# A two-layer decoder trunk on one NeuronCore: the fourth token sum of each FFN issued piece by piece in the first chain of the seven-product stage, one down-projection slot moved from the third chain to the end

## The chip, the cores and the metric

The kernel runs on one core of one Trainium2 chip. The metric is device time in microseconds (us), the median over several runs. Engines are named as in the profile: PE (TensorE matmul), PEld (its weight loads), DVE (VectorE), ACT (ScalarE), POOL (GpSimd), SP (SyncE, which here only issues transfers). Each engine takes its own instructions in the order in which they were issued.

## The reference

Two layers over 512 tokens of width 1024, in float32. Layer 0 mixes tokens by dilated attention, layer 1 by a gated linear recurrence; behind each mixer comes a gated convolutional FFN, and RMS norms stand around every part. The change touches the FFN only:

```python
def conv_ffn(x, w_up, conv_w, conv_b, w_down):
    u = causal_dwconv(x @ w_up, conv_w, conv_b)      # width 2 * 3072, a convolution of 3 tokens
    g, v = u[..., :D_FF], u[..., D_FF:]
    return (jax.nn.gelu(g, approximate=True) * v) @ w_down

def reference(x, ...):
    for layer in range(2):
        ...
        h = rms_norm(x, norm_ffn_pre[layer])
        h = conv_ffn(h, ffn_w_up[layer], ffn_conv_w[layer], ffn_conv_b[layer], ffn_w_down[layer])
        x = x + rms_norm(h, norm_ffn_post[layer])
    return x
```

## The kernel before

**Split products.** Every float32 operand is split into a high part (a copy by ACT, L149) and a low part (raw minus high, by DVE, L150). A product is then three matmuls: high by high, high by low, low by high.

**Two stages of the up-projection.** The 12 column blocks of the up-projection have two halves of 256 columns each, the gate half and the value half. Blocks 0 and 1 are done plainly (`feat_tiles`, `tiles`, matmuls of L412). Blocks 2 to 11 are done in `seven` as 20 *chains*, one for each half block. A chain multiplies a 2 by 2 arrangement of weight blocks and token blocks with seven products instead of eight; that needs sums of weight blocks and sums of token blocks. The four token sums are made once in each FFN by `token_sums`, a generator that is advanced by one step at each tick: `whole` adds high and low part again (tiles `B`, L938), differences follow (L944, L956, L963), and `parted` splits the result into the tiles `T` (ACT L149, DVE L150). The fourth sum, `T[3]`, is read by one product only, number 4.

**Slots.** The order of work in `seven` is written out by hand. A chain has ten places, `CYCLE = 10`, and the next chain starts ten places later; `AT = {1: 0, 5: 1, 2: 2, 6: 4, 3: 5, 7: 8, 4: 13}` gives the place of each product, so product 4 of a chain falls between two products of the next one. A place with something in it is a slot, called by its number m: m = 0 is product 1 of the first chain, m = 4 its product 6, m = 5 its product 3, m = 8 its product 7, m = 13 its product 4. A product is 12 matmuls with 256 columns (L1022). The places 6 and 7 of each chain (for the first two chains place 7 alone), and two places behind the last chain, hold `rows`: a part of the down-projection, 6 matmuls with 512 columns (L412, tiles `acc`). `free_slots` lists these 40 places, and the 40 parts are laid on them in order.

**What a slot issues.** `slot` issues the slot's matmuls, then what earlier slots left to be done `later`, then a `tick`. A tick first advances the generators on the side (`token_sums` here) and then, unless `state["hold"]` is set, calls `pump`, which splits the next weight piece (ACT L149, tiles `whi`; DVE L150, tiles `wlo`). In this stage a tick pumps one piece. `state["live"]` counts the piece buffers in use, of 16. The list of pieces has also the DVE additions that form the weight sums, `across` (L210) and `lower` (L214), and the transfers by POOL that add to a weight block (L186).

**What the seven products leave.** The products 1, 6, 7 and 4 of a chain add up in one half of a PSUM bank, 5, 3 and 2 in another bank. Behind the products 1, 6 and 5 ACT copies the running sum out into a tile `part` (L1031) before the next product is added onto it: so product 6 waits for the copy behind product 1, product 7 for the copy behind product 6, and product 3 for the copy behind product 5. DVE adds `part` to the finished bank (L1035 for the upper half of the result, L1040 for a part of the lower one; product 4 waits for L1040), and then come the bias (ACT L773), two taps of the convolution (DVE L777), and the gelu (ACT L795) or the gate (DVE L799).

**Ticks of the token sums.** Twelve ticks pass in blocks 0 and 1; the slots of `seven` go on counting. In the kernel before, the twelfth tick issues `whole` and both differences of the fourth sum (L938 twice, L944 twice), and the tick of slot m = 0 issues its two splits.

Of the kernel before, what the change touches and what calls it, by code (L numbers as in the profile page):

```python
# [32 lines left out]
HALVES = 16  # L33
# [8 lines left out]
CYCLE = 10  # L42
# [41 lines left out]
def kernel(  # L84
# [63 lines left out]
    def split(hi, lo, raw):  # L148
        nc.scalar.activation(hi, raw, AF.Copy)  # L149
        nc.vector.tensor_tensor(lo, raw, hi.bitcast(F32), op=ALU.subtract)  # L150
# [41 lines left out]
    def free_slots(n):  # L192

        end = CYCLE * n
        free = [CYCLE * c + r for c in range(n) for r in ((6, 7) if c > 1 else (7,))] + [end, end + 1]
        assert not {CYCLE * c + a for c in range(n) for a in AT.values()} & set(free)
        return free

# [104 lines left out]
    def pump(limit=2):  # L303

        for _ in range(limit):
            if not pieces:
                refill()
            while pieces and pieces[0][0] is None:
                pieces.pop(0)[1]()
            if not pieces or pieces[0][0][0] >= state["dma"]:  # L310
                continue
            if state["live"] + 2 - single(pieces[0][0][1]) <= HALVES:
                key, cuts, last = pieces.pop(0)
                cuts = cuts()
                his, los = [], []
                for n, raw in enumerate(cuts):
                    hi, lo = (
                        wp.tile([P] + list(raw.shape[1:]), F32R, tag=t, name=nm("w" + t)) for t in ("hi", "lo")
                    )
                    split(hi, lo, raw)  # L320
                    his.append(hi)
                    los.append(lo)
                units[key] = (his, los)
                state["live"] += len(cuts)
                state["used"] += last
                while pieces and pieces[0][0] is None:
                    pieces.pop(0)[1]()
            while not state["quiet"] and state["dma"] < len(plan) and state["dma"] - state["used"] < RAW_BUFS:
                load()
# [35 lines left out]
    def slot(emit, length=1):  # L365
        emit()
        for d in list(due):
            d[0] -= 1
            if d[0] < 0:
                due.remove(d)  # L370
                d[1]()
        tick(length)
# [544 lines left out]
    def token_sums(hT, T, first=False):  # L917

        if not first:
            assert len(sides) == 1, len(sides)  # L920
            d = dp.tile([P, 4, D], F32, name=nm("x_kept"))
            nc.gpsimd.dma_start(d, X[0])
            kept.append(d)
        homes = cp.tile([P, 4, D], F32R, tag="x_sb", name=nm("T"))
        homes = [homes[:, n] for n in range(4)]
        homes += [cp.tile([P, D], F32R, tag="gain", name=nm("T"), bufs=2) for _ in range(1 if first else 2)]
        homes = [[h[:, 0:512], h[:, 512:1024]] for h in homes]
        if first:
            homes += [[gen(F32R, "T") for _ in range(2)]]
        homes += [[wp.tile([P, 512], F32R, tag=t, name=nm("T")) for _ in range(2)] for t in ("hi", "lo")]  # L930
        state["live"] += 2
        homes = [[h.rearrange("p (k t) -> p k t", k=2) for h in hs] for hs in homes]
        yield 1 + first

        def both(k0, n):
            o = gen(s="B").rearrange("p (k t) -> p k t", k=2)
            hi, lo = (h[:, k0 : k0 + 2, n * 256 : n * 256 + 256] for h in hT)
            tt(o, hi.bitcast(F32), lo.bitcast(F32), op=ALU.add)  # L938
            return o

        tt = nc.vector.tensor_tensor

        def negative(o, a, b):
            nc.vector.scalar_tensor_tensor(o, a, -1.0, b, op0=ALU.mult, op1=ALU.subtract)  # L944

        def whole(k0, n):
            return [both(k0 + 2 * k, n) for k in range(2)]

        def parted(n, b):
            for k in range(2):  # L950
                split(homes[2 * n][k], homes[2 * n + 1][k], b[k])

        b11, b12 = whole(0, 0), whole(0, 1)
        yield 1 + first
        for k in range(2):
            tt(b11[k], b11[k], b12[k], op=ALU.subtract)  # L956
        parted(0, b11)
        yield 1 + first
        b22 = whole(4, 1)
        if not first:  # L960
            yield 1
        for k in range(2):
            tt(b12[k], b22[k], b12[k], op=ALU.subtract)  # L963
            negative(b22[k], b11[k], b22[k])
        yield 1 + first
        parted(1, b22)
        T.extend([homes[2 * n], homes[2 * n + 1]] for n in range(4))
        yield 1 + first
        parted(2, b12)
        yield 1 + first  # L970
        b21 = whole(4, 0)
        if first:
            yield 2
        for k in range(2):
            negative(b21[k], b22[k], b21[k])
        yield 1 + first
        parted(3, b21)

    LEFT = {5: ("s1", 1), 1: ("w11", 0), 3: ("s4", 1), 2: ("w12", 0), 6: ("s2", 1), 7: ("s3", 1), 4: ("a22", 1)}

# [65 lines left out]
    def seven(hT, T, begin, prep):  # L1046

        right = rights(hT, T)
        i0, acc, ends_at = state["next"], {}, CYCLE * 2 * len(SEVEN)

        def finish(b, ps, j, minus=False):
            later(2, begin(b, ps, j, minus, True))

        def ends(j, half):
            return (
                lambda ps: later(0, lambda: finish(2 * half, ps, j)),
                lambda ps: finish(2 * half + 1, ps, j, True),
            )

        def rows(k, pair):  # L1060
            W, A = take(i0, ("rows", k)), take(i0, ("act", k))
            for t in pair:
                if t not in acc:
                    acc[t] = psum("acc")
                mm3(acc[t], [a[0][:, t * P : (t + 1) * P] for a in A], [w[0] for w in W], not k, False)
            if pair[-1] == 3:
                done(2)

        fill = [lambda k=k, p=p: rows(k, p) for k in range(REST[0]) for p in ((0, 1), (2, 3))]
        steps = {}  # L1070
        n = 0
        for j in SEVEN:
            for half in range(2):
                f = chain(right, *ends(j, half))
                steps.update((CYCLE * n + AT[p], f(p)) for p in AT)
                n += 1
        free = free_slots(n)
        assert len(free) == len(fill)
        steps.update(zip(free, fill))
        state["even"] = True  # L1080
        for m in range(max(steps) + 1):
            if m == ends_at - 2:
                prep()
            if m in steps:
                slot(steps[m])
        while due:
            slot(lambda: None)
        done(2)
        state["even"] = False
        return acc  # L1090
# [626 lines left out]
```

## Time and profile before

| | |
|---|---|
| median of 3 runs | 1430.27 us (1430.02 to 1430.35) |
| the profiled execution: its own time | 1431.97 us |
| its span | 1430.1 us |
| mean granted PE clock | 0.994 |
| PE busy | 1405.7 us (98% of the span) |
| DVE busy | 1140.5 us (80%) |
| ACT busy | 800.2 us (56%) |
| POOL busy | 235.4 us (16%) |
| `seven` of layer 0, first product to the end of the last | 535.85 to 800.58 us |
| `seven` of layer 1, the same | 1081.68 to 1346.56 us |

Rows of the timeline read: start, length, engine, line, operation, output<-input, count, and in brackets how long the engine sat idle before it and for what. Rows of the chain of waits read: start, length, what. Rows of the windows give for each stretch its length, then for PE, PEld, DVE, ACT and POOL the busy time and (in brackets) the number of instructions, then the granted PE clock (1.00 is full), the share of the DMA engines and GB/s.

### The profile page before, as it was taken

The page shows a single profiled execution, that of the slowest core. Times are in us where ns is not written, and L with a number is a line of the kernel's source. Part 1 is how long each engine was busy: PE and PEld are TensorE (multiplying, and loading weights), DVE is VectorE, ACT ScalarE, POOL GpSimd, SP SyncE. Part 2 cuts the span into 40 slices and gives each one's busy share as a digit, 9 for nine tenths or more (in the row PEclk, how much of TensorE's full clock was granted, in tenths as well). Part 3 has the DMA queues.
Part 4 walks back from the last instruction along what each step waited for, and adds up shares of the span by engine and source line. Part 5 has one row for each costly group of instructions (what it writes and reads, how often), then busy time and mean ns, then how long its engine had stood idle before and what let it go on. Part 6 is the DMA issues. An engine that isn't in the chain of part 4 may idle for free.

```text
span 1430.1 us, 23824 instructions
## 1 busy us (share of the span) xinstructions
PE 1405.7 (98%) x8885; PEld 1275.0 (89%) x8885; DVE 1140.5 (80%) x2229; ACT 800.2 (56%) x1670; POOL 235.4 (16%) x352
## 2 busy tenths in 40 slices
PE   9999999999999998999999999999998999999997
PEld 7888999999998888999999889888897999999886
DVE  6676898787855988988888758779789898888843
ACT  7343555363636555666666555588455656666641
POOL 0341333130400211222110001000101112211000
PEclk9999999999999999999999999999999999999999
DMA  7553455664756545666664632432354666665511
GB/s 225 180 146 105 131 166 151 171 178 144 190 171 218 167 116 108 153 155 148 148 125 119 221 118 89 134 117 89 119 155 93 137 147 155 147 151 119 183 57 59
DMA packets 176108, 204.03 MB, mean 143 GB/s; under 512 B 10688, under 2 KB 145304, under 8 KB 175736
## 3 DMA queue, kind: packets, MB, share of 16 engines
q1 hardware_dynamic: 123064, 153.34, 33.5%
q0 software_dynamic: 52080, 48.11, 18.7%
q8 instruction: 70, 1.15, 0.3%
q10 hardware_dynamic: 848, 1.05, 0.2%
q14 instruction: 46, 0.38, 0.1%
HBM read 183.51 MB, written 18.96 MB: 142 GB/s over the span
## 4 chain that ended last, share of the span: by engine, by line
PE 84%; DVE 9%; ACT 5%; issue 1%; DMA 1%; POOL 0%; DVEq 0%; SPq 0%; ACTq 0%
PE ps L1022 38%; PE acc L412 24%; PE ps L412 9%; PE v L1215 7%; DVE wlo L150 2%; DVE u L777 2%; PE v L1153 1%; DVE xb L1520 1%; ACT whi L149 1%; PE O L1427 1%; PE S L1361 1%; PE S L1309 1%; DVE B L938 1%; ACT sig L1541 1%; PE tr L502 1%
## 5 line engine op out<-in xcount | busy, mean ns | idle before, releaser
L150 DVE TENSOR_TENSOR wlo<-raw,whi 128x512 fp32r<-128x512 f32 x632 | 417.5, 686 | 111.8 <-ACT whi L149 109.0
L149 ACT ACTIVATE whi<-raw 128x512 fp32r<-128x512 f32 x632 | 371.3, 625 | 141.9 <-PE ps L1022 45.9
L1022 PE MATMUL ps<-T,whi 128*128 128x256 f32 x1792 | 329.6, 284 | 14.8 <-ACT part L1031 11.0
L1022 PEld LDWEIGHTS ps<-T,whi 128*128 128x128 f32 x1792 | 280.6, 191 | 20.6 <-ACT part L1031 11.4
L1022 PE MATMUL ps<-T,wlo 128*128 128x256 f32 x896 | 252.0, 281 | 0.0
L1022 PE MATMUL ps<-hT,whi 128*128 128x256 f32 x1344 | 250.1, 284 | 0.0
L412 PE MATMUL ps<-hT,whi 128*128 128x512 f32 (+1 forms) x960 | 248.3, 348 | 0.0
L1022 PEld LDWEIGHTS ps<-hT,whi 128*128 128x128 f32 x1344 | 210.7, 192 | 0.8
L1022 PE MATMUL ps<-hT,wlo 128*128 128x256 f32 x672 | 190.9, 284 | 0.0
L412 PEld LDWEIGHTS ps<-hT,whi 128*128 128x128 f32 x960 | 167.6, 189 | 22.2
L186 POOL DMA_DIRECT2D raw<-in_ffn_w_up_dram x80 | 102.9, 1312 | 455.5 <-DVE wlo L150 337.2
L1022 PEld LDWEIGHTS ps<-T,wlo 128*128 128x128 f32 x896 | 171.5, 191 | 0.0
L412 PE MATMUL ps<-hT,wlo 128*128 128x512 f32 (+1 forms) x480 | 166.4, 347 | 0.0
L412 PE MATMUL acc<-whi,ahi 128*128 128x512 f32 x352 | 137.4, 390 | 0.0
L412 PE MATMUL acc<-whi,alo 128*128 128x512 f32 x352 | 137.2, 390 | 0.2
L412 PE MATMUL acc<-wlo,ahi 128*128 128x512 f32 x352 | 137.0, 389 | 0.0
L1022 PEld LDWEIGHTS ps<-hT,wlo 128*128 128x128 f32 x672 | 129.5, 193 | 0.0
L1031 ACT ACTIVATE part<-ps 128x256 f32<-128x256 f32 x168 | 63.8, 380 | 96.1 <-PE ps L1022 91.1
L1215 PE MATMUL v<-whi,hT 128*128 128x512 f32 x320 | 106.5, 396 | 0.0
L412 PEld LDWEIGHTS ps<-hT,wlo 128*128 128x128 f32 x480 | 90.8, 189 | 11.4
L777 DVE SCALAR_TENSOR_TENSOR u<-ps,cols,u 128x511 f32<-128x511 f32 x112 | 83.6, 746 | 4.9 <-ACT u L773 2.9
L773 ACT ACTIVATE u<-ps,cols 128x512 f32<-128x512 f32 x56 | 43.5, 776 | 70.8 <-DVE ps L1035 64.5
(206 smaller groups left out, 2165.3 us busy)
## 6 DMA issues: line engine op xcount, KB each, us to landing
raw<-in_ffn_w_up_dram SPq DMA_DIRECT2D x48, 1024.0 KB
raw<-in_attn_w_qkv_dram SPq DMA_DIRECT2D x67, 512.0 KB
raw<-in_ffn_w_up_dram POOLq DMA_DIRECT2D x80, 256.0 KB, 4.8
raw<-in_ffn_w_down_dram SPq DMA_DIRECT2D x14, 1024.0 KB
dw<-in_ffn_w_down_dram SPq DMA_DIRECT2D x40, 256.0 KB
raw<-in_lru_w_in_dram SPq DMA_DIRECT2D x8, 1024.0 KB
turned<-T POOLq DMA_DIRECT2D x26, 256.0 KB, 2.6
ft<-turned POOLq DMA_DIRECT2D x104, 64.0 KB, 4.4
```

Of the source, the lines that this page charges most:

```text
L149: nc.scalar.activation(hi, raw, AF.Copy)
L150: nc.vector.tensor_tensor(lo, raw, hi.bitcast(F32), op=ALU.subtract)
L186: nc.gpsimd.dma_start(to, src, accum_op=ALU.add)
L412: mm(dst, l[a], r[b], start=start and n == 0, stop=stop and n == 2)
L502: nc.tensor.transpose(ps[:, k * P : (k + 1) * P], xs[i][:, k * P : (k + 1) * P], ident)
L773: nc.scalar.activation(u, ps, AF.Identity, scale=own[:, j : j + 1], bias=cc[:, 48 + j : 49 + j])
L777: nc.vector.scalar_tensor_tensor(u[:, d:], ps[:, : S - d], wc, u[:, d:], op0=ALU.mult, op1=ALU.add)
L938: tt(o, hi.bitcast(F32), lo.bitcast(F32), op=ALU.add)
L1022: mm(dst, W[wa][0][:, k, :], right[n](ha, k), start=n in (1, 5) and k == q == 0, stop=k == 3 and q == 2, skip_group_check=True,)
L1031: later(1, lambda: nc.scalar.activation(to, dst, AF.Copy))
L1153: mm(banks[t], hT[a][:, k, t * P : (t + 1) * P], W[b][k % 2][:, 0, :], start=u == n == 0, stop=u == 3 and n == 5,)
L1215: mm(bank, hT[a][:, k, t * P : (t + 1) * P], W[b][k % 2][:, 0, :], start=(k, a, b) == (0, 0, 0), stop=(k, a, b) == (KD - 1, 1, 0),)
```

## The change

Three things, in both FFN layers:

1. In `token_sums` (for the FFN only; the attention's call, `first=True`, issues what it did) the two differences and the two splits of the fourth sum are no longer issued two at a time at the twelfth tick and the tick of m = 0. They go out one by one: the differences at m = 2 and m = 5, the splits at m = 8 and m = 11. In each of these four ticks `hold` is set, so no weight piece is split there.
2. `free_slots` gives the third chain one place for `rows` instead of two (place 26 goes), and there is a third place behind the last chain. All later parts of `rows` stand one place further on, their pieces and loads with them.
3. From m = 25 on, a slot whose number divides by five pumps one piece more, as long as fewer than 14 piece buffers are in use.

```diff
@@ free_slots @@
-        free = [CYCLE * c + r for c in range(n) for r in ((6, 7) if c > 1 else (7,))] + [end, end + 1]
+        free = [CYCLE * c + r for c in range(n) for r in ((6, 7) if c > 2 else (7,))] + [end, end + 1, end + 2]
@@ token_sums @@
         b21 = whole(4, 0)
+        yield 2 if first else 3
+        for k in range(2):
+            if not first:
+                state["hold"] = True
+            negative(b21[k], b22[k], b21[k])
+            if not first:
+                yield 1
+                state["hold"] = False
+                yield 1
         if first:
             yield 2
+            parted(3, b21)
+            return
         for k in range(2):
-            negative(b21[k], b22[k], b21[k])
-        yield 1 + first
-        parted(3, b21)
+            state["hold"] = True
+            split(homes[6][k], homes[7][k], b21[k])
+            yield 1
+            state["hold"] = False
+            yield 1
@@ seven @@
             if m in steps:
                 slot(steps[m])
+                if m > 2 * CYCLE and m % 5 == 0 and state["live"] < HALVES - 2:
+                    pump(1)
```

ACT at the start of `seven` in layer 0, from the first product on (`T1199` and `T1200` are the high parts of `T[3]`, `part1252` and `part1253` before, `part1251` and `part1252` now, are the copies behind the first chain's products 1 and 5, the second row of the first of them the one behind product 6; `u` is a convolution result). Before:

```order
L149 ACTIVATE whi1246_6296<-raw1189_5928 128x512
L149 ACTIVATE whi1249_6302<-raw1189_5928 128x512
L149 ACTIVATE T1199_5997<-B1244_6290 128x512
L149 ACTIVATE T1200_5998<-B1245_6292 128x512
L149 ACTIVATE whi1254_6326<-raw1133_5649 128x512
L1031 ACTIVATE part1252_6320<-ps1251_6307 128x256
L149 ACTIVATE whi1258_6348<-raw1207_6009 128x512
L1031 ACTIVATE part1253_6321<-ps1257_6334 128x256
L149 ACTIVATE whi1260_6366<-raw1189_5928 128x512
L149 ACTIVATE whi1262_6383<-raw1189_5928 128x512
L1031 ACTIVATE part1252_6320<-ps1251_6307 128x256
```

Now (the lines stand 13 further down, L1031 is L1044):

```order
L149 ACTIVATE whi1246_6294<-raw1189_5928 128x512
L149 ACTIVATE whi1248_6298<-raw1189_5928 128x512
L149 ACTIVATE whi1253_6318<-raw1133_5649 128x512
L1044 ACTIVATE part1251_6316<-ps1250_6303 128x256
L149 ACTIVATE whi1258_6342<-raw1207_6009 128x512
L1044 ACTIVATE part1252_6317<-ps1257_6328 128x256
L149 ACTIVATE whi1260_6373<-raw1189_5928 128x512
L1044 ACTIVATE part1251_6316<-ps1250_6303 128x256
L149 ACTIVATE whi1264_6401<-raw1189_5928 128x512
L773 ACTIVATE u1266_6417<-ps1257_6328,cols251_1206 128x512
L149 ACTIVATE T1199_5997<-B1244_6290 128x512
L149 ACTIVATE whi1270_6439<-raw1189_5928 128x512
```

The two splits into `T` stood ahead of the first copy `part`, and now stand behind the third one; `T1200` follows two rows below the last one shown, behind one more copy `part`. `whi1260`, which reads the result of the DVE addition L210, still stands ahead of the copy behind product 6.

DVE at the same place, from the fourth sum's `whole` on (`B1244` and `B1245`; `T1201` and `T1202` are the low parts of `T[3]`). Before:

```order
L938 TENSOR_TENSOR B1244_6290<-hT01043_5292,hT11044_5293 128x512
L938 TENSOR_TENSOR B1245_6292<-hT01043_5292,hT11044_5293 128x512
L944 SCALAR_TENSOR_TENSOR B1244_6290<-B1220_6123,B1244_6290 128x512
L944 SCALAR_TENSOR_TENSOR B1245_6292<-B1221_6125,B1245_6292 128x512
L150 TENSOR_TENSOR wlo1247_6297<-raw1189_5928,whi1246_6296 128x512
L150 TENSOR_TENSOR wlo1250_6303<-raw1189_5928,whi1249_6302 128x512
L799 TENSOR_TENSOR u1231_6202<-u1231_6202,u1243_6286 128x512
L150 TENSOR_TENSOR T1201_5999<-B1244_6290,T1199_5997 128x512
L150 TENSOR_TENSOR T1202_6000<-B1245_6292,T1200_5998 128x512
L150 TENSOR_TENSOR wlo1255_6327<-raw1133_5649,whi1254_6326 128x512
L210 TENSOR_TENSOR raw1189_5928<-raw1189_5928 128x4x128
```

Now, from behind `whole` (L1035 is L1048, L1040 is L1053):

```order
L150 TENSOR_TENSOR wlo1254_6319<-raw1133_5649,whi1253_6318 128x512
L210 TENSOR_TENSOR raw1189_5928<-raw1189_5928 128x4x128
L150 TENSOR_TENSOR wlo1259_6343<-raw1207_6009,whi1258_6342 128x512
L944 SCALAR_TENSOR_TENSOR B1244_6290<-B1220_6123,B1244_6290 128x512
L150 TENSOR_TENSOR wlo1261_6374<-raw1189_5928,whi1260_6373 128x512
L214 TENSOR_TENSOR raw1189_5928<-raw1189_5928 128x4x128
L944 SCALAR_TENSOR_TENSOR B1245_6292<-B1221_6125,B1245_6292 128x512
L1048 TENSOR_TENSOR ps1257_6328<-ps1257_6328,part1251_6316 128x512
L150 TENSOR_TENSOR wlo1265_6402<-raw1189_5928,whi1264_6401 128x512
L150 TENSOR_TENSOR T1201_5999<-B1244_6290,T1199_5997 128x512
L1053 TENSOR_TENSOR ps1250_6303<-ps1250_6303,part1252_6317 128x256
```

Between `whole` and `L210` eight instructions stood and now four (two `wlo`, L799 and `wlo1254`); behind the last row shown follow the two L777 of `u1266`, `wlo1271` and only then `T1202`.

PE at the end of `seven` in layer 0. Before, the last rows ahead of the last chain's product 4 (`T_5997` and `T_5999` are parts of `T[3]`):

```order
L412 MATMUL acc_6554<-whi_9267,whi_9285 128x512
L412 MATMUL acc_6554<-wlo_9268,whi_9285 128x512
L412 MATMUL acc_6554<-whi_9267,wlo_9286 128x512
L412 MATMUL acc_6558<-whi_9267,whi_9285 128x512
L412 MATMUL acc_6558<-wlo_9268,whi_9285 128x512
L412 MATMUL acc_6558<-whi_9267,wlo_9286 128x512
L1022 MATMUL ps_9289<-T_5997,whi_9305 128x256
L1022 MATMUL ps_9289<-T_5999,whi_9305 128x256
```

Ahead of these eight rows stand six more of L412 and then, before, the last chain's product 7. Now there are 18 rows of L412 between the products 7 and 4 instead of 12; the first of them are:

```order
L412 MATMUL acc_6537<-whi_9214,whi_9233 128x512
L412 MATMUL acc_6537<-wlo_9215,whi_9233 128x512
L412 MATMUL acc_6537<-whi_9214,wlo_9234 128x512
L412 MATMUL acc_6541<-whi_9214,whi_9233 128x512
L412 MATMUL acc_6541<-wlo_9215,whi_9233 128x512
L412 MATMUL acc_6541<-whi_9214,wlo_9234 128x512
L412 MATMUL acc_6392<-whi_9275,whi_9295 128x512
```

No instruction is added or removed on any engine, and the order on POOL and SP stays as it was.

## The prediction

> **What bounds the kernel now.** I read the page's busy shares and chain of waits first, then PE's waits, then the timeline where they lie.
>
> ```profile
> PE 1405.7 (98%) x8885; PEld 1275.0 (89%) x8885; DVE 1140.5 (80%) x2229; ACT 800.2 (56%) x1670; POOL 235.4 (16%) x352
> ...
> PE 84%; DVE 9%; ACT 5%; issue 1%; DMA 1%; POOL 0%; DVEq 0%; SPq 0%; ACTq 0%
> ```
>
> PE is busy for 98% of the span. The change neither adds nor removes matmuls, so it can win only PE's idle time (24 us) and stretches at a low clock. PE's waits, summed over the kernel (total, times, longest):
>
> ```profile
> PE ps L1022 <- ACT part L1031: 11.0, 2, 5.5
> PE ps L1022 <- DVE ps L1040: 3.8, 3, 1.3
> ```
>
> The wait of 5.5 us comes once in each FFN, at the start of `seven`, and one of 1.3 us once in each FFN at its end (the third is in the attention). The start in layer 0, from the timeline of PE, DVE and ACT:
>
> ```profile
> 537.61 1.14 ACT L149 ACTIVATE whi<-raw 128x512 fp32r<-128x512 f32 x2
> ...
> 540.01 0.28 PE L1022 MATMUL ps<-hT,wlo 128*128 128x256 f32 x1
> 540.34 1.53 DVE L777 SCALAR_TENSOR_TENSOR u<-ps,cols,u 128x511 f32<-128x511 f32 x2
> 541.78 1.28 DVE L938 TENSOR_TENSOR B<-hT,hT 128x512 f32<-128x512 f32 x2
> 542.99 1.29 DVE L944 SCALAR_TENSOR_TENSOR B<-B,B 128x512 f32<-128x512 f32 x2
> 543.70 1.23 ACT L149 ACTIVATE T<-B 128x512 fp32r<-128x512 f32 x2 [4.95 <-DVE B L944]
> 544.19 1.29 DVE L150 TENSOR_TENSOR wlo<-raw,whi 128x512 fp32r<-128x512 f32 x2
> 544.84 0.61 ACT L149 ACTIVATE whi<-raw 128x512 fp32r<-128x512 f32 x1
> 545.36 0.36 ACT L1031 ACTIVATE part<-ps 128x256 f32<-128x256 f32 x1
> ...
> 545.78 0.80 PE L1022 MATMUL ps<-T,whi 128*128 128x256 f32 x2 [5.49 <-ACT part L1031]
> ...
> 547.80 0.69 DVE L210 TENSOR_TENSOR raw<-raw 128x512 f32<-128x512 f32 x1
> ...
> 548.52 1.15 ACT L149 ACTIVATE whi<-raw 128x512 fp32r<-128x512 f32 x2 [2.00 <-DVE raw L210]
> ...
> 551.07 0.63 PE L412 MATMUL acc<-whi,whi 128*128 128x512 f32 x1
> ...
> 552.74 0.40 PE L1022 MATMUL ps<-T,whi 128*128 128x256 f32 x2
> ...
> 558.44 0.40 PE L1022 MATMUL ps<-T,whi 128*128 128x256 f32 x2
> ...
> 559.88 0.40 PE L1022 MATMUL ps<-T,whi 128*128 128x256 f32 x2
> ```
>
> ACT had nothing to do from 538.75 on but stood 4.95 us before the split of the fourth token sum, because DVE was late with its differences. The copy `part` behind product 1, which PE needs for product 6, stood behind that split. So a sum that is read only at m = 13 (558.44) held up product 6 at m = 4. Layer 1 shows the same:
>
> ```profile
> 1091.61 0.80 PE L1022 MATMUL ps<-T,whi 128*128 128x256 f32 x2 [5.49 <-ACT part L1031]
> ```
>
> The wait costs more than its length. Windows (PE busy, PEld, DVE, ACT, POOL, then the granted clock), and two rows of the chain of waits for a chain at full clock:
>
> ```profile
> 540.30:545.80 5.50, 0.02 (x1) 0.03 (x1) 5.46 (x10) 2.10 (x5) 0.00 (x0) 0.92 0.00 0
> 545.80:551.10 5.30, 5.30 (x25) 5.30 (x26) 5.18 (x9) 2.72 (x7) 1.28 (x1) 0.50 0.36 111
> ...
> 576.70:589.50 12.80, 12.80 (x98) 12.31 (x97) 11.47 (x20) 8.54 (x16) 2.77 (x3) 1.00 0.68 148
> ```
>
> ```profile
> 577.02 9.99 PE ps L1022 x84
> 587.01 2.75 PE acc L412 x12
> ```
>
> A product slot lasts 9.99/7 = 1.43 us at full clock, a slot of `rows` 2.75/2 = 1.38. From 545.78 to 552.74 lie two products and one `rows`: 6.96 us instead of 4.24, so 2.7 us went to half clock. The wait costs 5.49 + 2.7 = 8.2 us in each layer.
>
> **The change, part by part.** First the start. Nothing ahead of DVE's L938 at 541.78 changes. DVE moves on by 0.60 us for each 512-wide instruction (541.78 to 542.99 for two), by 0.72 for each L777 (540.34 to 541.78 for two).
>
> *Product 6* needs the copy behind product 1. On ACT only one `whi` now stands ahead of it after 538.75, so it is done by 538.75 + 0.6 + 0.4 = 539.8, ahead of PE's 540.29 (540.01 + 0.28). The old wait is gone, and with it the low clock.
>
> *Product 7* needs the copy behind product 6, which stands on ACT behind `whi1260`, which waits for DVE's L210. Ahead of L210 are now `whole` and four instructions instead of eight: L210 at 541.78 + 6 x 0.60 = 545.4, against 547.80. From L210 to `whi` it was 0.72 us (547.80 to 548.52), from a `whi` to the copy behind it 0.52 (544.84 to 545.36), from copy to PE 0.42 (545.36 to 545.78): product 7 can start at 547.05. PE would be there at 540.29 + 2 x 1.43 + 1.38 = 544.5. **A new wait of 2.5 us**, with ACT idle in it. Late behind it on ACT are the next piece and `u` of L773; PE's next user of those is the second chain, which is pushed back by the same 2.5 us.
>
> One more row is needed for the next step, `u` by its group (busy, mean ns of one):
>
> ```profile
> L773 ACT ACTIVATE u<-ps,cols 128x512 f32<-128x512 f32 x19 | 14.8, 780 | 32.2 <-DVE ps L1035 32.2
> ```
>
> *Product 4* of the first chain needs `T[3]`. On DVE stand behind L210, at 0.60 each: `wlo1259` 546.0, L944, `wlo1261`, L214, L944, L1048 at 549.0, `wlo1265`. ACT's `u` (L773) follows L1048 at 549.7 and takes 0.78 (780 ns), then `T1199` to 551.1; DVE then does `T1201` (551.15), L1053 (551.75, 0.33 to the next, as in the row at 798.58 below), two L777 to 553.55, `wlo1271`, and `T1202` from 554.15 to 554.85. PE reaches product 4 at 547.05 + 4 x 1.43 = 552.8; seven of its matmuls (0.12 each) run before the first that reads `T1202`, so it stands from 553.6 to 554.9: **1.3 us more**. It ends at 554.9 + 0.6 = 555.5. Before, the slot behind it began at 559.88.
>
> So each start wins 559.88 - 555.5 = **4.4 us** (8.2 less 2.5 and 1.3). I followed the pieces on into the third chain: the tightest is its product 3, split at m = 22 and used at m = 25, ready some 1.3 us early by the same steps. The four ticks without a piece cost nothing there, hidden behind the reserve; DVE is spared four `wlo` (2.4 us) just when it is late.
>
> The end of `seven`:
>
> ```profile
> 797.38 0.39 PE L412 MATMUL acc<-whi,wlo 128*128 128x512 f32 x1
> ...
> 798.58 0.42 DVE L1040 TENSOR_TENSOR ps<-ps,part 128x256 f32<-128x256 f32 x1
> 798.91 0.68 DVE L799 TENSOR_TENSOR u<-u,u 128x512 f32<-128x512 f32 x1
> 799.05 0.50 PE L1022 MATMUL ps<-T,whi 128*128 128x256 f32 x2 [1.29 <-DVE ps L1040]
> ...
> 800.58 0.40 PE L412 MATMUL acc<-whi,ahi 128*128 128x512 f32 x1
> ...
> 804.09 1.28 DVE L150 TENSOR_TENSOR alo<-u,ahi 128x512 fp32r<-128x512 f32 x2
> ...
> 1345.02 0.51 PE L1022 MATMUL ps<-T,whi 128*128 128x256 f32 x2 [1.28 <-DVE ps L1040]
> ```
>
> The last product 4 waits for L1040. The part of `rows` that is moved there takes 1.38 us, and DVE has the same instructions ahead of L1040 as before. It fills the gap, and the place that it left in the third chain is closed by the work behind it: 1.29 us less in each layer, less some 0.05. Two `wlo` now stand ahead of L799 on DVE, which delays the next `alo` by up to 1.2 us; those splits come at 804.1 before and PE reads them at 806.5 (800.58 and 24 matmuls of 0.23, and two more), so it is hidden. Without that cover it would cost up to 1.2 us in each layer.
>
> Sum: 2 x (4.4 + 1.25) = 11.3 us. Against the profiled execution: span 1430.1 to 1418.8, with the 1.9 us around it 1420.7; the median stands 1.7 us below that execution (1430.27 against 1431.97), so **1419.0 us**.
>
> **The clock behind the new wait.** The trace has no gap of 2.5 us. Below it stands the one of 1.29 us, around which the clock is full (the windows' row, clock behind POOL's column):
>
> ```profile
> 799.00:802.00 3.00, 2.95 (x19) 2.69 (x20) 3.00 (x6) 1.85 (x4) 0.00 (x0) 1.00 0.18 8
> ```
>
> Above it stands the gap of 5.49 us. In that, a mean clock of 0.92 over 5.5 us means half clock for 0.16 x 5.5 = 0.9 us, so it fell about 4.6 us into the gap. 2.5 us is well short of that, and I take full clock. If it fell all the same, product 7 and two more would run at half clock; product 4 would then end near 556.8, and each start win 3.1 us.
>
> [...] By a threshold under 2.5 us the sum would be 1421.6.
>
> **The rivals.**
> - *Half clock behind the new wait* (above): 2 x (3.1 + 1.25) = 8.7 us, 1421.6. For it: PE waits twice within 8 us. Against: 4.6 us. 14%.
> - *Only the end wins.* DVE is the true bound (5.46 of 5.50 us busy in the wait), and `T1202`, now behind two L777, comes another 4.4 us late, so that the start wins nothing: 1430.27 - 2.5 = 1427.8. Against: four `wlo` less ahead of it. 10%.
> - *No new wait:* L210 and `T1202` come in time, 2 x (8.2 + 1.25) = 18.9, 1411.4. It would need DVE 2.5 us faster from 541.78 to L210 than rows of 0.60 allow. 8%.
> - *Slower, from the fourth chain on.* Counting splits and releases slot by slot, 13 of 16 piece buffers were in use in every chain; the extra pieces raise that to 14. A `whi` then takes a buffer that PE freed only a slot or two ago, ACT stands, and DVE behind it. Now neither happens between 563 and 790 us; ACT's `whi` is in no wait for PE, and the waits there are
>
> ```profile
> ACT part L1031 <- PE ps L1022: 31.8, 25, 1.9
> ```
>
> ```profile
> DVE wlo L150 <- ACT whi L149: 22.7, 44, 0.8
> ```
>
>   DVE idles 22.7/18 = 1.26 us per chain. A wait for PE of 1.9 us (the longest) in each of 17 chains and two layers would take that and 0.64 us more: 22 us, 1441. It decides from 1.26 + 11.3/34 = 1.6 us per chain. Against: the copies behind it on ACT wait for the same slots anyway, and L1040 has over 3 us to spare in mid-stage by the same steps. 12%.
>
> **How the numbers follow.** The forecast has 56%: 1419.0, its own range 1416 to 1422 (0.7 us on each wait in each layer). The range for 8 in 10 reaches into the half-clock case and to near "only the end", and half way to "no new wait": 1414 to 1427. A measurement here can tell 0.2% (2.9 us) from no change. Faster by more: 56 + 14 + 8 + 4 = 82%; within it: half of "only the end" and some of the last, 7%; slower 11%.
>
> **What would show it.** Right: PE's wait for `part` at m = 4 is gone, one of about 2.5 us stands ahead of product 7 (m = 8) behind `whi` and L210, one of about 1.3 us inside product 4 for `T`; the clock is 1.00 from 536 to 560; no wait for L1053 at the ends; PE's waits in the two stages near 7.6 us in all. Wrong: a clock of 0.5 behind m = 8; waits of PE between the fourth chain and the end; `T1202` later than 555.5 on the same scale.

## The result, and the profile after

| | before | now |
|---|---|---|
| median | 1430.27 us (1430.02 to 1430.35) | 1421.19 us (1420.93 to 1421.70) |
| ratio | | 0.9938 (95%: 0.9915 to 0.9960) |
| the profiled execution, its span | 1431.97, 1430.1 us | 1421.70, 1419.9 us |
| `seven` of layer 0, first product to the end of the last | 264.73 us | 259.36 us |
| `seven` of layer 1 | 264.88 us | 259.70 us |
| mean granted PE clock | 0.994 | 0.998 |

The change is faster by 9.1 us, or 0.6%. The lines of PE's waits that concern `seven` (total, times, longest):

```profile
PE ps L1035 <- ACT part L1044: 5.0, 2, 2.5
PE ps L1035 <- DVE ps L1053: 1.9, 3, 1.3
PE ps L1035 <- DVE T L150: 0.9, 1, 0.9
```

The wait for the copy `part` is still there twice, but 2.5 us long instead of 5.5. Of the three waits for L1053 the one of 1.3 us is the attention's; the two others are 0.3 us each and new. The wait for `T` occurs once, not twice. Rows of the timeline of PE, ACT and DVE, layer 0 first (to 795.24), then layer 1:

```profile
540.17 0.40 PE L1035 MATMUL ps<-T,whi 128*128 128x256 f32 x2
...
545.43 0.68 DVE L210 TENSOR_TENSOR raw<-raw 128x512 f32<-128x512 f32 x1
546.14 0.63 ACT L149 ACTIVATE whi<-raw 128x512 fp32r<-128x512 f32 x1 [5.39 <-DVE raw L210]
546.68 0.36 ACT L1044 ACTIVATE part<-ps 128x256 f32<-128x256 f32 x1
547.10 0.51 PE L1035 MATMUL ps<-T,whi 128*128 128x256 f32 x2 [2.52 <-ACT part L1044]
...
552.90 0.40 PE L1035 MATMUL ps<-T,whi 128*128 128x256 f32 x2
...
554.08 0.68 DVE L150 TENSOR_TENSOR T<-B,T 128x512 fp32r<-128x512 f32 x1
554.82 0.39 PE L1035 MATMUL ps<-T,whi 128*128 128x256 f32 x1 [0.92 <-DVE T L150]
...
555.52 0.40 PE L1035 MATMUL ps<-T,whi 128*128 128x256 f32 x2
...
590.05 0.51 PE L1035 MATMUL ps<-T,whi 128*128 128x256 f32 x2 [0.31 <-DVE ps L1053]
...
795.24 0.40 PE L412 MATMUL acc<-whi,ahi 128*128 128x512 f32 x1
...
1087.55 0.50 PE L1035 MATMUL ps<-T,whi 128*128 128x256 f32 x2 [2.52 <-ACT part L1044]
...
1130.85 0.50 PE L1035 MATMUL ps<-T,whi 128*128 128x256 f32 x2 [0.32 <-DVE ps L1053]
...
1336.04 0.40 PE L412 MATMUL acc<-whi,ahi 128*128 128x512 f32 x1
```

Product 6 (540.17) starts without a wait. Product 7 waits 2.52 us, and behind it DVE, ACT and PE release each other in the order of the prediction: L210, `whi`, `part`, matmul. Product 4 starts at 552.90, stands for the second low part of `T[3]` and ends at 555.52. There is no wait at either end of the stage. In layer 1 there is no wait for `T`, and the reason is the clock. Windows of 3.41 us (length, then busy time and instructions of PE, PEld, DVE, ACT and POOL, granted clock, DMA share, GB/s), two in layer 0 and three in layer 1, each group around the wait of 2.52 us:

```profile
542.49:545.90 3.41, 2.08 (x12) 1.48 (x11) 3.41 (x7) 0.00 (x0) 0.00 (x0) 1.00 0.00 0
545.90:549.32 3.42, 2.22 (x18) 2.23 (x19) 3.42 (x7) 1.42 (x3) 1.27 (x1) 1.00 0.74 240
...
1085.21:1088.62 3.41, 1.07 (x9) 1.07 (x10) 3.41 (x7) 1.42 (x3) 1.16 (x1) 1.00 0.38 110
1088.62:1092.04 3.42, 3.42 (x19) 3.42 (x18) 2.65 (x5) 1.81 (x3) 0.42 (x2) 0.50 1.12 309
1092.04:1095.45 3.41, 3.41 (x30) 3.41 (x30) 3.14 (x6) 1.92 (x5) 0.99 (x1) 1.00 0.85 106
```

The same wait left the clock at 1.00 in layer 0 and brought it to 0.50 in layer 1, from 1088.62 to 1092.04. That is 1.07 us after PE had gone on working.

### The profile page after: what moved, and what is told of

Read it like the earlier page. It is cut to its first block, busy times and chain, and to the rows that moved or that the text cites. A ratio compares the mean times of both kernels' runs of the same rounds, so it can differ in the third digit from the quotient of the medians.

```text
span 1419.9 us, 23882 instructions
## 1 busy us (share of the span) xinstructions
PE 1402.4 (99%) x8885; PEld 1271.4 (90%) x8885; DVE 1139.2 (80%) x2229; ACT 799.9 (56%) x1670; POOL 235.2 (17%) x352
## 3 DMA queue, kind: packets, MB, share of 16 engines
q8 instruction: 70, 1.15, 0.3%
## 4 chain that ended last, share of the span: by engine, by line
PE 85%; DVE 7%; ACT 5%; issue 2%; DMA 1%; POOL 0%; DVEq 0%; SPq 0%; ACTq 0%
PE ps L1035 35%; PE acc L412 24%; PE ps L412 13%; PE v L1230 7%; DVE wlo L150 2%; ACT whi L149 1%; PE v L1168 1%; DVE xb L1535 1%; PE O L1442 1%; PE S L1376 1%; PE S L1324 1%; ACT sig L1556 1%; PE tr L502 1%; DVE u L777 1%; PE O L412 0%
## 5 line engine op out<-in xcount | busy, mean ns | idle before, releaser
L1035 PE MATMUL ps<-T,whi 128*128 128x256 f32 x1792 | 328.0, 283 | 7.9 <-ACT part L1044 5.0
L1035 PEld LDWEIGHTS ps<-T,whi 128*128 128x128 f32 x1792 | 279.3, 190 | 14.0 <-ACT part L1044 5.9
L1035 PE MATMUL ps<-T,wlo 128*128 128x256 f32 x896 | 251.4, 281 | 0.0
L1035 PE MATMUL ps<-hT,whi 128*128 128x256 f32 x1344 | 249.2, 284 | 0.0
L412 PE MATMUL ps<-hT,whi 128*128 128x512 f32 (+1 forms) x960 | 248.4, 349 | 0.0
L1035 PEld LDWEIGHTS ps<-hT,whi 128*128 128x128 f32 x1344 | 209.9, 192 | 0.8
L1035 PE MATMUL ps<-hT,wlo 128*128 128x256 f32 x672 | 190.6, 284 | 0.0
L412 PEld LDWEIGHTS ps<-hT,whi 128*128 128x128 f32 x960 | 167.6, 189 | 22.1
L1035 PEld LDWEIGHTS ps<-T,wlo 128*128 128x128 f32 x896 | 170.6, 190 | 0.0
L412 PE MATMUL ps<-hT,wlo 128*128 128x512 f32 (+1 forms) x480 | 166.6, 347 | 0.0
L412 PE MATMUL acc<-whi,ahi 128*128 128x512 f32 x352 | 137.7, 391 | 0.0
L412 PE MATMUL acc<-whi,alo 128*128 128x512 f32 x352 | 137.3, 390 | 0.2
L412 PE MATMUL acc<-wlo,ahi 128*128 128x512 f32 x352 | 137.2, 390 | 0.0
L1035 PEld LDWEIGHTS ps<-hT,wlo 128*128 128x128 f32 x672 | 129.1, 192 | 0.0
L1044 ACT ACTIVATE part<-ps 128x256 f32<-128x256 f32 x168 | 63.5, 378 | 75.8 <-PE ps L1035 75.3
L412 PEld LDWEIGHTS ps<-hT,wlo 128*128 128x128 f32 x480 | 90.9, 189 | 11.4
L777 DVE SCALAR_TENSOR_TENSOR u<-ps,cols,u 128x511 f32<-128x511 f32 x112 | 83.5, 745 | 4.9 <-ACT u L773 2.9
L463 POOL DMA_DIRECT2D ft<-turned x136 | 74.7, 557 | 32.2 <-issue 6.8
```

What stands on the lines that cost most here:

```text
L412: mm(dst, l[a], r[b], start=start and n == 0, stop=stop and n == 2)
L463: nc.gpsimd.dma_start(t[32 * c : 32 * c + 32].rearrange("j (b x) -> j b x", b=4), d.rearrange("(b j) (c x) -> c j b x", j=32, c=4)[c],)
L777: nc.vector.scalar_tensor_tensor(u[:, d:], ps[:, : S - d], wc, u[:, d:], op0=ALU.mult, op1=ALU.add)
L1035: mm(dst, W[wa][0][:, k, :], right[n](ha, k), start=n in (1, 5) and k == q == 0, stop=k == 3 and q == 2, skip_group_check=True,)
L1044: later(1, lambda: nc.scalar.activation(to, dst, AF.Copy))
```

## The experiments

The runs of this section were made in four groups, each beside runs of the kernel before, with medians of 1430.25, 1430.68, 1429.94 and 1430.96 us. A difference of two versions from different groups can be off by about as much as these differ.

### The change again

No edit.

> The changed kernel once more, word for word, as the yardstick of the runs beside it and for one more profile. In its first profile PE stood 2.52 us before product 7 in both layers; behind that the clock stayed full in layer 0 and fell to one half in layer 1, from 1088.7 to 1092.0. Theory: the clock is judged on a fixed beat of about 3.4 us that runs on without regard to the program, and falls when PE has idled for much of one beat, so that the same wait of 2.52 us halves it or not by chance of where the beat falls; then this profile may show it halved in either layer, both or none, with the same wait of 2.5 us, and times of 1420.5 to 1422. Rival: it is something of layer 1 (its transfers or what ran before); then this profile shows the same again, half clock behind the wait in layer 1 only, for about 3.3 us.

Measured: 1421.83 us (1421.56 to 1422.30). The stage took 259.70 us in layer 0 and 259.34 in layer 1, the reverse of the first profile. Windows of this run around the two waits:

```profile
544.75:548.16 3.41, 0.89 (x6) 0.46 (x5) 3.41 (x7) 1.37 (x3) 0.51 (x1) 1.00 0.19 46
548.16:551.60 3.44, 3.44 (x18) 3.44 (x17) 2.81 (x5) 1.24 (x3) 0.77 (x1) 0.50 1.03 329
...
1084.06:1087.47 3.41, 2.01 (x12) 1.40 (x10) 3.41 (x6) 0.00 (x0) 0.00 (x0) 1.00 0.00 0
1087.47:1090.88 3.41, 2.28 (x19) 2.28 (x20) 3.41 (x7) 1.42 (x3) 1.27 (x1) 1.00 0.78 254
```

Now layer 0 has the half clock and layer 1 has not, and the wait for `T` (0.90 us) moved to layer 1. So it is no property of a layer: the rival falls. Where the wait lay inside one beat (PE busy for 0.89 us of it), the clock fell at that beat's end; where it was cut in two (busy 2.01 and 2.28 us), it stayed.

### The parts of the change alone

Sums only: `free_slots` as before, no extra piece.

```diff
-        free = [... ((6, 7) if c > 2 else (7,))] + [end, end + 1, end + 2]
+        free = [... ((6, 7) if c > 1 else (7,))] + [end, end + 1]
...
-                if m > 2 * CYCLE and m % 5 == 0 and state["live"] < HALVES - 2:
-                    pump(1)
```

> The token sums one by one as in the change, the places of rows and the pumping as before the change. Theory (the parts add up): the starts win what they won in the change, so that product 4 of the first chain ends 19.6 to 20.0 us behind the first product, and the waits of 1.3 us at the two ends are back: about 1423.3 us, 1.9 to 2.5 above the change. Rival: the four ticks without a piece leave the reserve short where no piece is added later, and PE waits for pieces or copies between the second chain and the end: 1425 or more, with waits of PE for whi or wlo.

Measured: 1428.58 us (1426.88 to 1429.63). The rival's time is right, its place is not: PE waits nowhere between the second chain and the end, but at the end itself, for DVE:

```profile
796.08 0.50 PE L1035 MATMUL ps<-T,whi 128*128 128x256 f32 x2 [2.45 <-DVE ps L1053]
```

The wait of 1.29 us grew to 2.45 in both layers, and the clock was halved for one beat (3.41 us) behind it, from 797.38 to 800.80 in layer 0. The four `wlo` put off at the start came due here: on DVE two more than before stand ahead of L1053, and two more just behind it.

Slot only: the kernel before with the place of `rows` moved.

```diff
-        free = [... ((6, 7) if c > 1 else (7,))] + [end, end + 1]
+        free = [... ((6, 7) if c > 2 else (7,))] + [end, end + 1, end + 2]
```

> The kernel before with only the slot of rows moved to the end. Theory: it wins the two waits of 1.29 us and nothing else, 1430.27 less 2.5: about 1427.8 us; the wait of 5.49 us before product 6 stays in both layers, with half clock behind it for some time between 5.3 and 6.8 us that differs from one execution to the next by 3.4 us or parts of it. Rival: the gap opened in the third chain or the parts of rows that are one place late cost as much as they win: 1430.

Measured: 1427.80 us (1426.83 to 1428.75), as the theory said; no wait at either end. Its profile shows what the wait of 5.48 us does to the clock in another execution (layer 1, the wait ends at 1089.21):

```profile
1082.18:1085.59 3.41, 1.55 (x13) 1.34 (x12) 3.37 (x6) 0.00 (x0) 0.00 (x0) 1.00 0.00 0
1085.59:1089.00 3.41, 0.00 (x0) 0.00 (x0) 3.41 (x7) 1.87 (x4) 0.00 (x0) 1.00 0.00 0
1089.00:1092.44 3.44, 3.23 (x15) 3.23 (x16) 3.44 (x6) 1.44 (x4) 0.00 (x0) 0.50 0.03 6
```

The half clock lasted one beat, to 1092.44; in the profile of before it lasted two in each layer (544.88 to 551.70 and 1091.00 to 1097.84). A beat with PE busy for 1.55 us stayed at full clock.

The change without the extra pieces: only the two lines of `pump(1)` go.

> The change without the extra piece at every fifth slot. Theory: the extra pieces put more wlo ahead of L1053 and so caused the wait of 0.31 us before a product 4 in the fourth chain's time (590.05 in layer 0); without them that wait is gone and nothing else changes: about 1420.6 us. Rival: the extra pieces refill the reserve that the four ticks without a piece took; without them PE or ACT waits later in the stage, 1423 or more.

Measured: 1425.56 us (1425.01 to 1425.76), 3.7 above the change in the same group. Layer 0, PE:

```profile
794.22 0.48 PE L1035 MATMUL ps<-T,whi 128*128 128x256 f32 x2 [0.58 <-DVE ps L1053]
801.07 0.47 PE L412 MATMUL acc<-whi,ahi 128*128 128x512 f32 x1 [1.75 <-DVE u L777]
```

Both statements hold in part. The wait of 0.31 us at m = 33 is gone, as the theory said, but PE waits 0.58 us before the last product 4 and 1.75 us just behind the stage, in both layers. Six `wlo` stand ahead of the last L777 there instead of four. Twice (0.58 + 1.75 less 0.31) is 4.0 us; the spans differ by 4.1 (1424.0 and 1419.9). The extra pieces are what pays back the four ticks without a piece.

### Which wait decides at the start

Copy first: the second difference at m = 4, so that its tick without a piece falls there, and `whi1260` goes behind the copy of product 6.

```diff
-        for k in range(2):
-            if not first:
-                state["hold"] = True
-            negative(b21[k], b22[k], b21[k])
-            if not first:
-                yield 1
-                state["hold"] = False
-                yield 1
...
+        state["hold"] = True
+        negative(b21[0], b22[0], b21[0])
+        yield 1
+        state["hold"] = True
+        negative(b21[1], b22[1], b21[1])
+        yield 1
+        state["hold"] = False
+        yield 2
...
```

> The change with the second difference at m = 4 (and that tick without a piece) instead of m = 5, so that the piece whose high part waits for L210 is split one slot later and stands on ACT behind the copy of product 6, not ahead of it. The splits of the fourth sum stay at m = 8 and m = 11. Theory (DVE is late as a whole, and T[3] is what decides): the wait of 2.5 us before product 7 is gone, but the second low part of T[3] comes no sooner, some 18.9 us behind the first product, so that product 4 stands 3.5 to 4.2 us inside itself and ends 19.6 us behind the first product as before; nothing is won, and a single wait of that length leaves half clock behind it in at least one layer, which nothing absorbs now: 1421.8 plus 0 to 5, about 1424 us. Rival (the copy behind L210 on ACT is the limit): with it out of the way both starts win the 2.5 us: about 1417.

Measured: 1425.25 us (1424.05 to 1426.73), as the theory said. PE, layer 0 (first product at 535.11):

```profile
551.52 0.48 PE L1041 MATMUL ps<-T,whi 128*128 128x256 f32 x2 [2.02 <-DVE ps L1059]
...
554.06 0.39 PE L1041 MATMUL ps<-T,whi 128*128 128x256 f32 x1 [1.47 <-DVE T L150]
```

The wait before product 7 is gone, and product 4 waits for DVE, 2.02 + 1.47 = 3.49 us in place of 2.52 + 0.92 = 3.44. Only the name of the wait changed; DVE's queue sets the end of product 4. Standing later and closer together, these waits had the clock halved behind them in both layers (554.34 to 557.76 and 1093.65 to 1100.48), with nothing to absorb it.

Sum early: as copy first, the splits at m = 7 and m = 8.

```diff
         state["hold"] = False
-        yield 2
+        yield 1
         state["hold"] = True
         split(homes[6][0], homes[7][0], b21[0])
         yield 1
-        state["hold"] = False
-        yield 1
         state["hold"] = True
         split(homes[6][1], homes[7][1], b21[1])
...
```

> As the run with the copy first, and the two splits of the fourth sum at m = 7 and m = 8 instead of m = 8 and m = 11, these two ticks without a piece. Theory: the second low part of T[3] is done 15.1 to 15.8 us behind the first product (DVE has four instructions fewer ahead of it), product 4 stands some 0.7 us, ends about 16.5 us behind the first product instead of 19.6, and both starts win about 3 us; the pieces of chains 2 to 4 come under more pressure, and the wait before the product 4 at m = 33 grows from 0.31 us to 1 or 2: 1421.8 - 6 + 2, about 1418 us. Rival: DVE is behind by as much later, so that what the start wins is lost in full at the next three chains: 1421.5.

Measured: 1420.11 us (1419.43 to 1420.62), 1.7 below the change in the other group, half of what was expected. PE, layer 0:

```profile
551.76 0.47 PE L1039 MATMUL ps<-T,whi 128*128 128x256 f32 x2 [2.01 <-DVE ps L1057]
```

`T[3]` came in time, but product 4 now waited 2.0 us in each layer for L1057, the addition of `part`, which the theory had left out; the wait at m = 33 stood at 0.33 us in layer 0 and 0.80 in layer 1. The clock fell behind the wait of 2.0 us in layer 0 alone (552.12 to 555.53).

The four ticks with a piece too:

```diff
-                state["hold"] = True
+                state["hold"] = False
```

(in both places; each is passed twice).

> The change with the four ticks of the fourth sum splitting a weight piece too, as every other tick does. Theory (sparing DVE four wlo in the first chain is part of the gain): the second low part of T[3] has three or four more instructions of 0.6 us ahead of it, product 7 waits about 3.1 us and product 4 about 2.8 us, ends 21.8 us behind the first product instead of 19.6: 2 x 2.2 more, 1426 us, and up to 2 more where the clock falls behind the waits. Rival: the order on ACT alone made the gain; then the time is that of the change, 1421.8.

Measured: 1424.77 us (1424.30 to 1427.07), 2.9 above the change: the four ticks are part of the gain. PE, layer 0:

```profile
547.75 0.80 PE L1035 MATMUL ps<-T,whi 128*128 128x256 f32 x2 [3.06 <-ACT part L1044]
```

Product 7 waits 3.06 us as expected, half clock follows for two beats in both layers (546.85 to 553.68 in layer 0), and with that product 4 hardly waits for `T` (0.18 us in layer 0, nothing in layer 1).

### The debt paid later

Extra pieces from m = 60 on, one for each chain:

```diff
-                if m > 2 * CYCLE and m % 5 == 0 and state["live"] < HALVES - 2:
+                if m > 5 * CYCLE and m % 10 == 0 and state["live"] < HALVES - 2:
```

> The change with the extra pieces from m = 60 on and at every tenth number only, four or five of them instead of the same number between m = 25 and m = 40. Theory: the extra pieces are needed before the end of the stage, not early; the wait of 0.31 us at m = 33 goes away and the end stays without a wait: 0.6 us less than the change, about 1421.2. Rival: the reserve of 9 to 10 buffers is too thin for chains 4 to 6 and PE waits there: 1423.

Measured: 1420.11 us (1419.48 to 1420.60). PE's waits for L1053 are the attention's alone, so the two of 0.3 us were due to the early extra pieces:

```profile
PE ps L1035 <- DVE ps L1053: 1.2, 1, 1.2
```

The time is 1.7 us below the change, more than these 0.6 us. The two stages together are 0.7 us shorter than in the change's profile (518.3 against 519.1 us); where the rest comes from is open. The clock fell behind the wait before product 7 in both layers here (0.50 from 548.16 to 551.57 and from 1087.46 to 1090.88), and in neither does product 4 wait for `T`.

Sum early and pieces later together:

> The run with the sum early and the run with the pieces later in one kernel. Theory: the two are independent; the waits at m = 33 (0.33 and 0.80 us) go, the rest is that of the sum early: 1420.1 less 1.1, about 1419.0 us. Rival: the chains 2 to 4 are short of DVE time whichever piece stands there, and a wait of as much comes back at another product: 1420.1.

Measured: 1418.73 us (1417.19 to 1419.19). The gains add up nearly: 1.7 us each alone, 3.1 together, against the change. What is left at the start of layer 0, ACT, DVE and PE:

```profile
549.24 0.78 ACT L773 ACTIVATE u<-ps,cols 128x512 f32<-128x512 f32 x1 [1.78 <-DVE ps L1052]
549.91 0.62 ACT L149 ACTIVATE T<-B 128x512 fp32r<-128x512 f32 x1
...
549.10 0.69 DVE L150 TENSOR_TENSOR T<-B,T 128x512 fp32r<-128x512 f32 x1
550.56 0.69 DVE L150 TENSOR_TENSOR T<-B,T 128x512 fp32r<-128x512 f32 x1 [0.77 <-ACT T L149]
551.17 0.43 DVE L1057 TENSOR_TENSOR ps<-ps,part 128x256 f32<-128x256 f32 x1
...
551.74 0.47 PE L1039 MATMUL ps<-T,whi 128*128 128x256 f32 x2 [2.01 <-DVE ps L1057]
```

DVE, which is late, stands 0.77 us for the second high part of `T[3]`. ACT had nothing to do for 1.78 us, but that split stands behind `u`, which waits for DVE's L1052.

Splits sooner: the same with the splits at m = 5 and m = 7.

```diff
         negative(b21[1], b22[1], b21[1])
         yield 1
-        state["hold"] = False
-        yield 1
         state["hold"] = True
         split(homes[6][0], homes[7][0], b21[0])
```

> As the run before, with the splits of the fourth sum at m = 5 and m = 7 instead of m = 7 and m = 8 (four ticks in a row without a piece: m = 2, 4, 5, 7). In the run with the sum early it was no longer T[3] but L1057, the part added on DVE, that product 4 waited for, 2.0 us; here one wlo and one split less stand ahead of that addition. Theory (DVE's queue decides, instruction by instruction): product 4 starts some 15.4 us behind the first product, not 16.4; 1 us less in each layer: about 1417 us. Rival: what is put behind it (the pieces of the second chain, the copy that product 6 of the second chain needs) is then late by as much: 1419.

Measured: 1418.69 us (1417.38 to 1419.66): the rival's time. The expectation had miscounted: a `wlo` and the addition L214 now stand behind the splits, but still ahead of L1055, so the same instructions stand there in another order, and the gap on DVE (0.78 us, now at that `wlo`) is among them as before.

One more tick without a piece, at m = 1, in the kernel with the splits sooner:

```diff
-        yield 2 if first else 3
+        yield 2
+        if not first:
+            state["hold"] = True
+            yield 1
...
```

> As the run with the splits sooner, and the tick of m = 1 without a piece too, so that one more wlo stands behind the fourth sum on DVE. Theory: product 4 starts about 15.0 us behind the first product, and the second chain's products 6 and 3 wait some 0.8 us in all for their pieces, so that little more is won: 1416 to 1417 us. Rival: no wait comes back and each wlo put off wins its full 0.6 us: 1415.5; or the second chain stands for its pieces by more than was won: 1419.

Measured: 1422.14 us (1421.67 to 1422.19), worse than every expectation. In layer 0 product 4 ends 16.9 us behind the first product, against 18.6 with the splits sooner, yet the stage takes 260.1 us against 258.8. The second chain and those behind it stand for pieces, as this line of PE's waits shows:

```profile
PE ps L1040 <- DVE wlo L150: 3.3, 10, 0.8
```

Both splits at m = 7, in the kernel with the sum early and the pieces later; m = 8 still without a piece:

```diff
         split(homes[6][0], homes[7][0], b21[0])
-        yield 1
-        state["hold"] = True
         split(homes[6][1], homes[7][1], b21[1])
-        yield 1
+        yield 2
```

> As the run with the sum early and the pieces later, with both splits of the fourth sum at m = 7 (m = 8 still without a piece). DVE's order stays the same; on ACT the second high part of T[3] now stands ahead of the bias u (L773), which waits for L1050, not behind it. In the run before DVE stood 0.77 us for that high part. Theory: that gap goes, L1055 and with it product 4 come 0.77 us sooner, PE waits 1.24 us instead of 2.01; and 1.24 us is 36% of a beat of the clock, under the 54% that was seen to leave it full, so that no half clock follows in either layer where both had it in the last profile: 2 x 0.8 and up to 2 x 1.7 less than 1418.7, 1414.5 to 1416.5 us. Rival: DVE is only idle there because it is not short of time; product 4 starts where it did and the time is 1418.7.

Measured: 1415.69 us (1415.48 to 1415.93), ratio to before 0.9893 (0.9877 to 0.9910). This is the best version, 5.5 us below the change. ACT, DVE and PE in layer 0:

```profile
546.97 1.23 ACT L149 ACTIVATE T<-B 128x512 fp32r<-128x512 f32 x2 [0.57 <-DVE B L944]
...
549.26 1.29 DVE L150 TENSOR_TENSOR T<-B,T 128x512 fp32r<-128x512 f32 x2
550.46 0.43 DVE L1055 TENSOR_TENSOR ps<-ps,part 128x256 f32<-128x256 f32 x1
...
551.03 0.47 PE L1037 MATMUL ps<-T,whi 128*128 128x256 f32 x2 [1.15 <-ACT part L1046]
```

DVE's order is that of the kernel with the sum early and the pieces later; only two instructions on ACT changed places. The gap on DVE is gone, the wait is 1.15 us instead of 2.01 (put down to a copy that ended within 0.1 us of L1055), and the mean clock is 0.999 instead of 0.996: in layer 0 it was 1.00 from 535 to 560, where the kernel with the sum early and the pieces later had 0.50 from 552.65 to 556.06 and, in layer 1, from 1091.95 to 1095.37. So the gain is part shorter wait (0.86 us in each layer), part clock.

## Why the prediction was right, point by point

**Product 6, product 7, product 4 in layer 0: right, to a tenth.** Product 7 was placed at 547.05 and came at 547.10; its wait of 2.5 us is 2.52. The end of product 4 was put at 555.5 and is 555.52. The wait for `T` is listed with 0.92 us instead of 1.3; but product 4 took 2.62 us (552.90 to 555.52) instead of 1.43, so it cost 1.2. The walk along DVE's queue at 0.60 us for each instruction carried all of it. Copy first confirms the cause: with the named wait removed, the time is lost to DVE all the same.

**The ends: right.** Both waits of 1.3 us are gone, and alone the moved slot wins 2.5 us.

**"The four ticks without a piece cost nothing there, hidden behind the reserve": incomplete.** It is right for the start. But the reserve is only lent: without the extra pieces the four `wlo` come due at the end of the stage and cost 2 x (0.58 + 1.75) us. The prediction took "DVE has the same instructions ahead of L1040 as before" from the order of the whole change and did not say that the third part of the change makes it so.

**The rival "slower, from the fourth chain on": the mechanism is there, small.** It was priced at 1.9 us in every chain; what came is one wait of 0.31 us in each layer, at m = 33, and it goes when the extra pieces are spread over later chains. "L1040 has over 3 us to spare in mid-stage" failed in that one place.

**"2.5 us is well short of that, and I take full clock": failed.** In one of two layers the clock fell. The step read the fall in the old wait as a delay of 4.6 us from its beginning. In the runs the falls lie on a beat of 3.41 us instead, and for a wait of 2.52 us its place in the beat decided: in the two profiles of the change a beat with PE busy for 1.07 or 0.89 us of 3.41 lost the full clock, and those busy for 2.01 to 2.28 us kept it. The kernel was the same, and the clock fell at 1088.62, in layer 1, in one profile and at 548.16, in layer 0, in the other. The size was small by luck of place: the half clock delayed product 4 by 1.5 us, of which 1.2 would have been lost to `T` anyway, so that the layer lost 0.34 us (259.70 against 259.36), not the rival's 1.3. The rival's price does not follow from its own condition either: at half clock product 3 took 2.57 us in the profile of before (548.50 to 551.07), so three products would have cost 3 x (2.57 - 1.43) = 3.4 us and ended product 4 near 557.6, not 556.8.

**The sum.** The forecast for the profiled execution was a span of 1418.8; it is 1419.9. The two waits at m = 33 make 0.6 us of the difference, the half clock about 0.3, and the stretch behind `seven` of layer 1 took 0.3 longer (83.86 us against 83.54).

**"The median stands 1.7 us below that execution": the step that cost most.** It was carried over as a constant to the changed kernel, where the profiled execution stands only 0.5 us above the median: 1.2 of the 2.2 us by which 1419.0 was too low. The profile of before had half clock for 5.92 and 6.23 us behind the two waits (545.78 to 551.70 and 1091.61 to 1097.84). From product 6 to product 7 it took 6.96 and 7.09 us there, against 4.24 at full clock, so this cost 5.6 us. With the same waits, the profile of the slot alone had 3.96 and 3.23 us of half clock, and the same way took 6.09 and 5.76 us, costing 3.4. So the profile of before had caught a dearer execution, and what made it so was just what the change removes. That this makes up the whole spread of before is argued, not shown; it fits that before ranges over 2.9 us in the runs beside these (1429.47 to 1432.36), and the version with the splits together, with a mean clock of 0.999 in its profile, over 0.45 (four runs only).

## What to carry to other kernels

- The wait that a profile names can be only the last link: ask what the engine behind it (here DVE) still has to do before the next consumer, and walk its queue instruction by instruction. Moving the named instruction alone won nothing; on an engine with idle time, bringing an instruction ahead of one that waits for the late engine won 3.0 us, the clock's part included.
- Work that is put off at a crowded place has to be paid back somewhere: look where the reserve is refilled, and spread it over stretches where the late engine idles.
- One profile can give one draw of a stall's price (the wait of 2.52 us had half clock behind it in one layer of two, in layer 1 in one profile of the change and in layer 0 in the other); take a median over executions only for the kernel that it was measured on.

## What the runs showed of the hardware

In these traces the changes of the clock lie on a beat of 3.41 us. In the run with the sums only the clock fell (read in windows of 0.02 us) at 548.22, 797.39, 1090.94 and 1340.11; the last three falls lie 249.17, 542.72 and 791.89 us behind the first, or 73, 159 and 232 times 3.413 us, and each of the four half clocks lasted 3.41 us. Eleven profiles show falls in or just behind `seven`, 21 in all. These beats began at full clock and had a wait of PE in them (PE busy, of 3.41 us, and the clock of the next beat):

| run | next at 1.00 | next at 0.50 |
|---|---|---|
| before | 2.24, 2.13, 1.94, 2.13 | 0.00, 0.00 |
| the change | 2.08, 2.22 | 1.07 |
| the change again | 2.01, 2.28 | 0.89 |
| sums only | | 1.30 |
| slot only | 1.55 | 0.00 |
| copy first | | 1.39 |

So the nine in which PE was idle for up to 55% kept full clock, and the seven with 59% or more lost it, at the beat's end; for other beats this table shows nothing. The nearest on either side are the row with PE busy for 1.55 us above (kept) and this one of copy first (lost):

```profile
1090.22:1093.63 3.41, 1.39 (x13) 1.22 (x11) 2.64 (x6) 2.56 (x5) 0.92 (x1) 1.00 1.15 255
```

The half clock lasted one beat or two: in the profile of before, one with PE busy for 2.81 of 3.42 us had a second one at half clock behind it, while one of the run with the sums only, busy for 2.93 of 3.41 us, had full clock behind it (rows in this order):

```profile
1091.00:1094.42 3.42, 2.81 (x13) 2.81 (x14) 3.42 (x7) 1.42 (x5) 0.00 (x0) 0.50 0.02 5
...
1090.94:1094.35 3.41, 2.93 (x13) 2.93 (x14) 3.41 (x7) 1.21 (x4) 1.27 (x1) 0.50 1.01 301
```

By the length of the wait: that of 1.75 us (no extra pieces) left the clock at 1.00 in both layers; of those of 2.0 to 2.52 us some had half clock behind them and some had not (2.0 us in sum early and 2.52 us in the change: one layer each); and those of 3.06 us (no tick without a piece) and 5.5 us (before and slot only) had half clock behind them in both, for one beat or two.
